# Forgetting attention in pairs of heads with its key bias by DRAM and GpSimd, and the S5 rotation on GpSimd

## The chip, the cores and the metric

The kernel runs on one core of a Trainium2 chip. Its time is the device time of one execution in microseconds (us), given as the median of several executions. A core has a matrix engine (PE, TensorE; its weight loads are shown apart as PEld), three elementwise engines (DVE or VectorE, ACT or ScalarE, POOL or GpSimd) and a queue engine (SP) that here issues every DMA. Each engine runs its own instruction list in order and waits on semaphores for the others. SBUF is the on-chip memory, PSUM the matrix engine's accumulators, DRAM the memory outside.

## The reference, cut to what matters

The network has three blocks on 256 tokens of width 1024. The change touches the third block's mixer, which adds three branches: forgetting attention ("fox"), a state-space recurrence ("s5") and a gated recurrence ("hgrn"). Fox has 8 heads of 64 features; its score gets a bias from a running sum of log forget gates, and is causal:

```python
c = jnp.cumsum(log_f, axis=1)                     # per head
s = jnp.einsum('bqhd,bkhd->bhqk', qi, k) * scale
s = s + ci[..., None] - c_keys                    # query bias, minus key bias
s = jnp.where(k_pos[None, :] <= q_pos[:, None], s, -jnp.inf)
p = jax.nn.softmax(s, axis=-1)
return jnp.einsum('bhqk,bkhd->bqhd', p, v)
```

The recurrence of s5 is complex, state by state, over the 256 tokens:

```python
h[t] = abar * h[t-1] + bbar @ u[t]                # complex
y[t] = Re(c @ h[t])
```

## The kernel before, in words

Weights are loaded in units of 1 MB into a tile `raw` (three buffers). ACT writes the high part `wh`, DVE the remainder `wl` (method `unit`, lines 366, 360, 351 are the helpers that issue matmul, tensor_tensor and activation), and PE does three products for each, `wh` with the high and the low part of the activations and `wl` with the high part. A unit is 48 products of 256 columns. These products are most of the kernel.

The mixer of the third block (`mixer2`) writes the steps of `M2_ORDER`, "su fox hz hv g2 g0 b0 glu dr g1 b1 b2": the projections, and between them side generators (fox, hgrn, s5) that are advanced a piece at a time. A scheduler puts the instructions of each engine into one fixed order when the kernel is built. Projections accumulate in PSUM tiles `mm`, everything else in four tiles `ax`.

**s5.** 16 groups of 128 states, two groups (`j`) in each of 8 steps (`p`). Per group: PE makes the drive `dp` (tile `ax<-su,s5bt`; the two groups sit in different 32-row strips); DVE multiplies it by cos and sin tables (`s5tl`, loaded from DRAM), adds, and scans the real and the imaginary part along time (`s5w<-mag,merged`), which is a recurrence in a rotating frame. Then the result is rotated back, one 128x512 product with sin into `merged` and one with cos in place in `s5w`, both on DVE. After every second step PE multiplies the four groups with the output matrix `s5c` (`ax<-s5w,s5c`, `ax<-merged,s5c`).

**fox.** The log gates and their running sum `c` live on 32 partitions (tiles `fr`); `cn` is its negative, `cc` holds `c` turned so that the query is on the partitions. Head by head (`step(h)`): for the query tiles t=0 (128 keys) and t=1 (256 keys), PE makes the scores (`ax<-fx`, 64 rows of contraction) and adds the key bias by a second product of 32 rows (`ax<-fr,cst`, a row of the identity against `cn`). ACT adds the query bias and copies to SBUF tile `qt`; DVE adds the causal mask and takes the row maximum in one instruction (line 1636); ACT does exp; DVE scales; PE transposes the probabilities (`ax<-cst,qt`) and multiplies them with the values (`ax<-qt,fx`, 64 columns of output). `lagged` issues the scores of a head before the transposes of the head before it. `qt` has four buffers.

PE's weights for a product on 64 or 32 rows fill only part of the array; products in different row strips or column strips can stand side by side in it.

Of the kernel before, what the change touches and what calls it, by code (L numbers as in the profile page):

```python
# [11 lines left out]
F32 = mybir.dt.float32  # L12
F32R = mybir.dt.float32r
I32 = mybir.dt.int32
AF = mybir.ActivationFunctionType
ALU = mybir.AluOpType
# [3 lines left out]
P = 128  # L20
D = 1024
T = 256
# [246 lines left out]
class Stack:  # L269
# [1109 lines left out]
    def s5(self, us):  # L1379

        nc = self.nc
        bt = self.pt("s5bt", [P, 2, 4, P])
        nc.sync.dma_start(out=bt.rearrange("p a b c -> p (a b c)"), in_=self.s5bt)
        cc = self.pt("s5c", [P, 3, 16, 32])
        nc.sync.dma_start(out=cc[:, 0:2].rearrange("p a b c -> p (a b c)"), in_=self.a["c5"])
        self.act(cc[:, 2], cc[:, 0], scale=-1.0)
        self.act(cc[:, 1], cc[:, 1], scale=-1.0)
        held = []

        def step(p):  # L1390


            f = p // 2
            u = us[f // 2][:, f % 2]
            js = (2 * p, 2 * p + 1)
            tabs, dps = [], []
            for j in js:
                tab = self.pt("s5tl", [P, 2, T], bufs=2)
                nc.sync.dma_start(out=tab, in_=self.s5tab[j].rearrange("p (a b) -> p a b", a=2))
                tabs.append(tab)  # L1400
                dps.append(self.ax((P, 2, T)))
            first = None
            for c in range(2):
                for j, dp in zip(js[::-1], dps[::-1]):
                    b = 32 * (j % 4)
                    first = self.after(first, self.matmul(dp[:, c], bt[b:b + 32, c, f], u[b:b + 32]))
            for j, tab, dp in zip(js, tabs, dps):
                w1 = self.pt(f"merged{j % 4}", [P, 2, T])
                w2 = self.pt("s5w2", [P, 2, T], bufs=4)
                cob = tab[:, 0].unsqueeze(1).to_broadcast([P, 2, T])  # L1410
                sib = tab[:, 1].unsqueeze(1).to_broadcast([P, 2, T])
                self.tt(w1, dp, cob, ALU.mult)
                self.tt(w2, dp, sib, ALU.mult)
                self.tt(w1[:, 0], w1[:, 0], w2[:, 1], ALU.add)
                self.tt(w1[:, 1], w1[:, 1], w2[:, 0], ALU.subtract)
                mg = self.mag[:, j:j + 1].to_broadcast([P, T])
                for c in range(2):
                    self.scan(w2[:, c], mg, w1[:, c], 0.0, ALU.mult, ALU.add)
                self.tt(w1, w2, sib, ALU.mult)
                self.tt(w2, w2, cob, ALU.mult)  # L1420
                held.append((j, w1, w2))

        def outputs(f):
            u = us[f // 2][:, f % 2]
            yp = self.ax((P, 512))[:, 0:T]

            first = None
            for i in range(4):
                for j, w1, w2 in held[::-1]:
                    b = 32 * (j % 4)  # L1430
                    c, w = ((0, w2[:, 0]), (2, w1[:, 1]), (1, w1[:, 0]), (1, w2[:, 1]))[i]
                    first = self.after(first, self.matmul(yp[b:b + 32], cc[:, c, j], w, i == 0, i == 3))
            held.clear()
            self.stt(u, u, self.col("s5d", f), yp, ALU.mult, ALU.add)

        for p in range(8):
            step(p)
            yield
            if p % 2:
                outputs(p // 2)  # L1440
            yield

        zh = self.pt("s5bt", [P, 4, T], F32R)
        zl = self.pt("s5c", [P, 4, T], F32R)
        a_ = []
        for i in range(2):
            y = us[i]
            a = self.pt("s5w2", [P, 2, T], bufs=4)
            a_.append(a)
            self.tt(a, y, y, ALU.mult)  # L1450
            self.ts(a, a, 0.044715 * GELU_C, GELU_C, ALU.mult, ALU.add)
            self.tt(a, a, y, ALU.mult)
            self.act(a, a, AF.Tanh)
            self.ts(a, a, 0.5, 0.5, ALU.mult, ALU.add)
            self.tt(y, y, a, ALU.mult)
            self.split(zh[:, 2 * i:2 * i + 2], zl[:, 2 * i:2 * i + 2], y)
        self.s5z = (zh, zl, us, a_)
        yield
# [145 lines left out]
    def fox(self, qkv):  # L1604
        nc = self.nc
        fp = self.ax()[0:32, 0:T]
        self.proj_rows("ff", fp)
        z, lf, na, c, cn = (self.pt(f"fr{i}", [32, T]) for i in range(5))
        self.ts(z, fp, self.col("fb", rows=32), None, ALU.add)
        self.log_sigmoid(lf, z, na)  # L1610
        self.scan(c, self.ones[0:32], lf, 0.0, ALU.mult, ALU.add)
        self.ts(cn, c, -1.0, None, ALU.mult)
        cp = self.ax((P, 4, P))
        for t in range(2):
            self.transpose(cp[:, t, 0:32], c[:, t * P:(t + 1) * P])
        cc = self.pt("fcc", [P, 2, 32])
        self.act(cc, cp[:, 0:2, 0:32])
        yh, yl = self.pt("fyh", [P, 4, T], F32R), self.pt("fyl", [P, 4, T], F32R)
        yield
        yp = []  # L1620

        def step(h):
            if len(qkv) < 3 * (h // 4) + 3:
                return True
            q, k, v = qkv[3 * (h // 4):3 * (h // 4) + 3]
            b, f = 64 * (h % 2), (h % 4) // 2
            sp = self.ax((P, 2, T))
            s = self.qt([P, 2, T])
            m, nm, su, rs = (self.sm(2, f"fs{i}") for i in range(4))
            for t in range(2):  # L1630
                w = (t + 1) * P
                mask = self.mB[:, P:] if t == 0 else self.mB
                self.matmul(sp[:, t, 0:w], q[b:b + 64, f, t * P:(t + 1) * P], k[b:b + 64, f, 0:w], True, False)
                self.matmul(sp[:, t, 0:w], self.ident[0:32, h:h + 1].to_broadcast([32, P]), cn[:, 0:w], False, True)
                self.act(s[:, t, 0:w], sp[:, t, 0:w], AF.Identity, bias=cc[:, t, h:h + 1])
                nc.vector.tensor_tensor_reduce(out=s[:, t, 0:w], in0=s[:, t, 0:w], in1=mask, scale=1.0, scalar=-3.0e38,
                                               op0=ALU.add, op1=ALU.max, accum_out=m[:, t:t + 1])
            self.ts(nm, m, -1.0, None, ALU.mult)
            for t in range(2):
                w = (t + 1) * P  # L1640
                self.act(s[:, t, 0:w], s[:, t, 0:w], AF.Exp, bias=nm[:, t:t + 1], accum_out=su[:, t:t + 1])
            nc.vector.reciprocal(out=rs, in_=su)

            def rest():
                tp = self.ax((P, 2, T))
                for t in range(2):
                    w = (t + 1) * P
                    self.ts(s[:, t, 0:w], s[:, t, 0:w], rs[:, t:t + 1], None, ALU.mult)
                    for kt in range(t + 1):
                        self.transpose(tp[:, kt, t * P:(t + 1) * P], s[:, t, kt * P:(kt + 1) * P])  # L1650
                pt = self.qt([P, 2, T])
                self.act(pt[:, 0], tp[:, 0])
                self.act(pt[:, 1, P:], tp[:, 1, P:])
                if h % 2 == 0:
                    yp.append(self.ax()[:, 0:T])
                hs = slice((h % 4) * 64, (h % 4 + 1) * 64)
                y = yp[-1]
                self.matmul(y[b:b + 64], v[:, 0, hs], pt[:, 0], True, False)
                self.matmul(y[b:b + 64, P:], v[:, 1, hs], pt[:, 1, P:], False, True)
                if h % 2:  # L1660
                    self.split(yh[:, h // 2], yl[:, h // 2], y)
            return rest

        yield from self.lagged([partial(step, h) for h in range(8)])
        self.yb[0] = (yh, yl)

    def mixer2(self, tick, nb=1):
# [275 lines left out]
```

## Time and profile before

| | |
|---|---|
| median of 3 runs | 1518.69 us (1518.07 to 1520.74) |
| the profiled execution | 1525.01 us, span 1523.2 us |
| PE busy | 1458.0 us |
| PEld busy | 1311.8 us |
| DVE busy | 1163.0 us |
| ACT busy | 855.7 us |
| POOL busy | 4.5 us |

The span runs from the first to the last instruction of the profiled execution; 1.8 us of its own time lie outside. Everything below is read from that one execution, and times of the trace count from the start of the span. The third block's mixer lies between about 936 and 1260 us.

### The profile page before, as it was taken

To read this page: it belongs to the slowest core of one execution; us is meant where nothing else is said; L and a number is where in the kernel's file an instruction comes from. 1 tells how busy PE (TensorE), PEld (TensorE's weight loads), DVE (VectorE), ACT (ScalarE), POOL (GpSimd) and SP (SyncE) were. 2 spreads that over 40 slices of the span, in tenths; PEclk is the share of its full clock that TensorE was granted. 3 is DMA by queue.
4 is the path that set the end of the run, shared out by engine and by line. 5 is a ranking of instruction groups with operands and counts; after the bars stand their busy time and mean duration, and the time that the engine had idled before them with its cause. 6 is when DMAs were issued, how large, how long until landed. Compare 5 with 4: busy or idle time off the path is not lost.

```text
span 1523.2 us, 25378 instructions
## 1 busy us (share of the span) xinstructions
PE 1458.0 (96%) x9964; PEld 1311.8 (86%) x9964; DVE 1163.0 (76%) x2223; ACT 855.7 (56%) x1502; POOL 4.5 (0%) x24
## 2 busy tenths in 40 slices
PE   2998999999999899999999999999999999999999
PEld 2987887898998899998889989967889989799998
DVE  7788988877778896667988856958999887565555
ACT  4786774654556565545757665535455457444443
POOL 0000000000000000000000000000000000000000
PEclk8999999999999999999999999969999999999999
DMA  8755887487875794436676655522344365245552
GB/s 347 262 167 171 292 307 265 189 313 282 318 294 200 291 315 158 166 139 211 230 263 227 242 217 192 173 97 89 133 142 149 132 224 198 83 150 182 194 181 97
DMA packets 62058, 315.47 MB, mean 207 GB/s; under 512 B 6385, under 2 KB 15217, under 8 KB 28146
## 3 DMA queue, kind: packets, MB, share of 16 engines
q1 hardware_dynamic: 61938, 313.85, 57.9%
q8 instruction: 78, 1.28, 0.3%
q14 instruction: 42, 0.34, 0.1%
HBM read 304.77 MB, written 9.05 MB: 206 GB/s over the span
## 4 chain that ended last, share of the span: by engine, by line
PE 74%; DVE 14%; ACT 5%; DMA 5%; issue 2%; SPq 0%; ACTq 0%; DVEq 0%
PE mm L366 48%; PE ax L366 23%; DVE wl L360 3%; PE ax L370 2%; ACT xn L351 1%; DMA bp<-cs_d 1%; ACT wh L351 1%; DVE merged L360 1%; ACT nb L351 1%; DMA grow<-in_rows 1%; DVE acc L751 1%; DVE s5w L373 1%; DVE s5w L360 1%; DMA bp<-nM_d 1%; DMA x<-in_x 1%
## 5 line engine op out<-in xcount | busy, mean ns | idle before, releaser
L360 DVE TENSOR_TENSOR wl<-raw,wh 128x1024 fp32r<-128x1024 f32 x400 | 485.5, 1223 | 198.0 <-ACT wh L351 197.3
L351 ACT ACTIVATE wh<-raw 128x1024 fp32r<-128x1024 f32 x400 | 419.4, 1057 | 359.6 <-PE mm L366 209.4
L366 PE MATMUL mm<-xh,wh 128*128 128x256 f32 x1536 | 442.3, 288 | 5.7 <-ACT bp L351 3.1
L366 PE MATMUL mm<-xh,wl 128*128 128x256 f32 x1536 | 441.7, 288 | 5.6 <-DVE wl L360 5.6
L366 PE MATMUL mm<-xl,wh 128*128 128x256 f32 x1536 | 439.9, 286 | 0.0
L366 PEld LDWEIGHTS mm<-xh,wl 128*128 128x128 f32 x1536 | 298.0, 194 | 12.2 <-DVE wl L360 7.4
L366 PEld LDWEIGHTS mm<-xh,wh 128*128 128x128 f32 x1536 | 298.3, 194 | 11.4 <-ACT bp L351 3.3
L366 PEld LDWEIGHTS mm<-xl,wh 128*128 128x128 f32 x1536 | 298.2, 194 | 3.8 <-issue 2.0
L366 PE MATMUL mm<-wh,xh 128*128 128x256 f32 x496 | 143.9, 290 | 0.0
L366 PE MATMUL mm<-wl,xh 128*128 128x256 f32 x496 | 142.5, 287 | 0.5 <-DVE wl L360 0.5
L366 PE MATMUL mm<-wh,xl 128*128 128x256 f32 x496 | 141.7, 286 | 0.0
L366 PE MATMUL ax<-wh,mhh 128*128 128x512 f32 x256 | 102.4, 400 | 0.0
L366 PE MATMUL ax<-wl,mhh 128*128 128x512 f32 x256 | 101.4, 396 | 0.0
L366 PE MATMUL ax<-wh,mhl 128*128 128x512 f32 x256 | 101.3, 396 | 0.0
L366 PEld LDWEIGHTS mm<-wl,xh 128*128 128x128 f32 x496 | 95.8, 193 | 3.2 <-DVE wl L360 2.2
L366 PEld LDWEIGHTS mm<-wh,xh 128*128 128x128 f32 x496 | 95.7, 193 | 1.9 <-issue 1.2
L366 PEld LDWEIGHTS mm<-wh,xl 128*128 128x128 f32 x496 | 95.8, 193 | 1.0 <-issue 0.8
L366 PEld LDWEIGHTS ax<-wh,mhl 128*128 128x128 f32 x256 | 48.1, 188 | 11.9 <-DVE mhl L360 0.4
L366 PEld LDWEIGHTS ax<-wl,mhh 128*128 128x128 f32 x256 | 48.1, 188 | 10.9 <-issue 0.5
L366 PEld LDWEIGHTS ax<-wh,mhh 128*128 128x128 f32 x256 | 48.2, 188 | 10.7 <-ACT wh L351 0.5
L363 DVE SCALAR_TENSOR_TENSOR acc<-raw,cond,acc 128x1024 f32<-128x1024 f32 x28 | 35.8, 1278 | 8.1 <-DMA raw<-in_ada 7.9
L751 DVE CUSTOM_DVE_ANT_0 acc<-raw,crow 128x1024 f32<-128x1024 f32 x32 | 39.0, 1219 | 2.6 <-DMA raw<-in_ada 2.3
(490 smaller groups left out, 2543.2 us busy)
## 6 DMA issues: line engine op xcount, KB each, us to landing
raw<-in_wts SPq DMA_DIRECT2D x214, 1024.0 KB, 4.9
raw<-in_ada SPq DMA_DIRECT2D x48, 1024.0 KB, 5.6
nb<-in_nab SPq DMA_DIRECT2D x16, 256.0 KB, 5.8
grow<-in_rows SPq DMA_DIRECT2D x16, 256.0 KB, 6.0
bp<-cs_d SPq DMA_DIRECT2D x16, 256.0 KB, 5.2
s5tab<-s5t SPq DMA_DIRECT2D x16, 256.0 KB, 2.5
s5tl<-s5tab SPq DMA_DIRECT2D x16, 256.0 KB, 2.7
meml<-mem_d SPq DMA_DIRECT2D x2, 1024.0 KB, 5.2
```

The source lines that it names most:

```text
L351: return self.nc.scalar.activation(out=out, in_=in_, func=func, **kw)
L360: return self.nc.vector.tensor_tensor(out=out, in0=in0, in1=in1, op=op)
L363: return self.nc.vector.scalar_tensor_tensor(out=out, in0=in0, scalar=s, in1=in1, op0=op0, op1=op1)
L366: return self.nc.tensor.matmul(out, lhsT, rhs, start=start, stop=stop)
L370: return self.nc.tensor.transpose(out, in_, self.ident[0:k, 0:k])
L373: return self.nc.vector.tensor_tensor_scan(out=out, data0=d0, data1=d1, initial=init, op0=op0, op1=op1)
L751: nc.vector.tensor_tensor_reduce(out=acc, in0=w, in1=self.crow, scale=1.0, scalar=0.0, op0=ALU.mult, op1=ALU.add, accum_out=s8[:, j:j + 1])
```

## The change

Fox now works on pairs of heads (`pair(g)`, heads 2g and 2g+1). The key bias no longer is a PE product: `cn` is written to DRAM once (`cn_d`, 8 rows of 256), and for each head its row is read back to all 128 partitions (`fcb`, two buffers); ACT adds the query bias to it and writes `qt`; GpSimd adds the causal mask on the two 128x128 blocks on the diagonal; DVE adds scores and bias and takes the maximum in one instruction, which now reads the scores from PSUM. The scores of the two heads are issued alternately, head 1 (rows 64 to 127) before head 0 (rows 0 to 63), and so are the products with the values (columns 64 to 127, then 0 to 63). The pair's scores and softmax come in one piece, its transposes and value products in the next, and the following pair after that. In s5 the two products of the rotation back are issued on GpSimd.

```diff
-                self.tt(w1, w2, sib, ALU.mult)
-                self.tt(w2, w2, cob, ALU.mult)
+                for out, rot in ((w1, sib), (w2, cob)):
+                    nc.gpsimd.tensor_tensor(out=out, in0=w2, in1=rot, op=ALU.mult)
                 held.append((j, w1, w2))
...
-        z, lf, na, c, cn = (self.pt(f"fr{i}", [32, T]) for i in range(5))
+        z, lf, na = (self.pt(f"fr{i}", [32, T]) for i in range(3))
         self.ts(z, fp, self.col("fb", rows=32), None, ALU.add)
         self.log_sigmoid(lf, z, na)
+        c, cn = z, na
         self.scan(c, self.ones[0:32], lf, 0.0, ALU.mult, ALU.add)
         self.ts(cn, c, -1.0, None, ALU.mult)
+        cnd = self.tc.dram_tile([8, T], F32, name="cn_d")
+        nc.sync.dma_start(out=cnd, in_=cn[0:8])
...
-                self.matmul(sp[:, t, 0:w], q[b:b + 64, f, t * P:(t + 1) * P], k[b:b + 64, f, 0:w], True, False)
-                self.matmul(sp[:, t, 0:w], self.ident[0:32, h:h + 1].to_broadcast([32, P]), cn[:, 0:w], False, True)
-                self.act(s[:, t, 0:w], sp[:, t, 0:w], AF.Identity, bias=cc[:, t, h:h + 1])
-                nc.vector.tensor_tensor_reduce(out=s[:, t, 0:w], in0=s[:, t, 0:w], in1=mask, scale=1.0, scalar=-3.0e38,
-                                               op0=ALU.add, op1=ALU.max, accum_out=m[:, t:t + 1])
...
+                cb = self.pt("fcb", [P, T], bufs=2)
+                nc.sync.dma_start(out=cb, in_=cnd[h].partition_broadcast(P))
+                s = self.qt([P, 2, T])
+                for t in range(2):
+                    self.act(s[:, t, 0:(t + 1) * P], cb[:, 0:(t + 1) * P], AF.Identity, bias=cc[:, t, h:h + 1])
+                ends = s.rearrange("p t n -> p (t n)").rearrange("p (i n) -> p i n", n=P)[:, 0:4:3]
+                nc.gpsimd.tensor_tensor(out=ends, in0=ends, in1=self.mB[:, P:].unsqueeze(1).to_broadcast([P, 2, P]), op=ALU.add)
+                ss.append(s)
+                sp.append(self.ax((P, 2, T)))
             for t in range(2):
...
+                for i in (1, 0):
+                    b, w = 64 * i, (t + 1) * P
+                    first = self.after(first, self.matmul(sp[i][:, t, 0:w], q[b:b + 64, f, t * P:(t + 1) * P], k[b:b + 64, f, 0:w]))
...
                 for t in range(2):
                     w = (t + 1) * P
-                    self.ts(s[:, t, 0:w], s[:, t, 0:w], rs[:, t:t + 1], None, ALU.mult)
+                    nc.vector.tensor_tensor_reduce(out=s[:, t, 0:w], in0=sp[i][:, t, 0:w], in1=s[:, t, 0:w], scale=1.0, scalar=-3.0e38,
+                                                   op0=ALU.add, op1=ALU.max, accum_out=m[:, t:t + 1])
...
+            for kt in range(2):
+                for i in (1, 0):
+                    b, hs, w = 64 * i, slice((2 * f + i) * 64, (2 * f + i + 1) * 64), slice(kt * P, T)
+                    first = self.after(first, self.matmul(y[b:b + 64, w], v[:, kt, hs], pts[i][:, kt, w], kt == 0, kt == 1))
```

The built order shows what stands where. On PE, at the first scores of fox (`ax<-fx` scores, `ax<-fr,cst` key bias, then the first output products of s5), before:

```order
L370 MATMUL ax<-cst,qksq 128x128 x4
L366 MATMUL ax<-fx 128x128
L366 MATMUL ax<-fr_10690,cst 128x128
L366 MATMUL ax<-s5w_10809,s5c 32x256
L366 MATMUL ax<-s5w_10799,s5c 32x256
```

and at the same place after the change:

```order
L370 MATMUL ax<-cst,qksq 128x128 x4
L366 MATMUL ax<-fx 128x128 x2
L366 MATMUL ax<-fx 128x256 x2
L366 MATMUL ax<-s5w_10809,s5c 32x256
L366 MATMUL ax<-s5w_10799,s5c 32x256
```

The four score products of two heads stand together and the bias products are gone. Some 30 rows later on PE, where the softmax of the first pair is used (`ax<-cst,qt` transposes, `ax<-qt,fx` value products, `mm` projection products), after the change:

```order
L370 MATMUL ax<-cst,qt 128x128
L366 MATMUL mm<-xh,wh 128x256
L370 MATMUL ax<-cst,qt 128x128 x2
L366 MATMUL mm<-xl,wh 128x256
L366 MATMUL mm<-xh,wl 128x256
L366 MATMUL ax<-fx 128x128 x2
L366 MATMUL ax<-qt,fx 64x256 x2
L366 MATMUL ax<-qt,fx 64x128 x2
L366 MATMUL ax<-fx 128x256 x2
L366 MATMUL ax<-su_10329,s5bt 128x256 x4
```

Behind this place 96 projection products follow in one piece; between the first scores and here there are 14 in all. Before the change 21 projection products stood between the first scores and the drive products of the same s5 step, and 46 behind them.

On DVE, in the first step of s5 (`s5w<-mag,merged` scan, `merged<-s5w,s5tl` and `s5w<-s5w,s5tl` rotation back, `fr` gates of fox), before:

```order
L373 SCALAR_TENSOR_TENSOR s5w_10575<-mag,merged_10574 128x256 x2
L360 TENSOR_TENSOR merged_10584<-merged_10584,s5w_10585 128x256
L360 TENSOR_TENSOR merged_10574<-s5w_10575,s5tl 128x512
L373 SCALAR_TENSOR_TENSOR s5w_10585<-mag,merged_10584 128x256
L360 TENSOR_TENSOR s5w_10575<-s5w_10575,s5tl 128x512
L373 SCALAR_TENSOR_TENSOR s5w_10585<-mag,merged_10584 128x256
L356 TENSOR_SCALAR fr_10686<-ax,cols 32x256
L360 TENSOR_TENSOR merged_10584<-s5w_10585,s5tl 128x512
L363 SCALAR_TENSOR_TENSOR fr_10688<-fr_10686 32x256
L360 TENSOR_TENSOR s5w_10585<-s5w_10585,s5tl 128x512
L360 TENSOR_TENSOR wl<-raw,wh 128x1024 x2
```

and after:

```order
L373 SCALAR_TENSOR_TENSOR s5w_10575<-mag,merged_10574 128x256 x2
L360 TENSOR_TENSOR merged_10584<-merged_10584,s5w_10585 128x256
L356 TENSOR_SCALAR fr_10686<-ax,cols 32x256
L373 SCALAR_TENSOR_TENSOR s5w_10585<-mag,merged_10584 128x256 x2
L363 SCALAR_TENSOR_TENSOR fr_10688<-fr_10686 32x256
L360 TENSOR_TENSOR wl<-raw,wh 128x1024
```

The four rotations left DVE's list, and fox's gates and the next `wl` moved up. They stand on POOL, whose list after the change is four rotations for each s5 step, the masks of fox (two instructions for a pair) between them, and one memset pair that hgrn's scan waits for.

## Rows read from the trace of the kernel before

**Rows 1.** The page, part 1: busy us, share of the span, instructions

```profile
PE 1458.0 (96%) x9964; PEld 1311.8 (86%) x9964; DVE 1163.0 (76%) x2223; ACT 855.7 (56%) x1502; POOL 4.5 (0%) x24
```

**Rows 2.** Windows: stretch, its us, busy of each engine, PEclk, DMA share

```profile
960.00:1002.40 42.40, 40.24 (x329) 37.76 (x331) 38.66 (x78) 19.56 (x27) 0.00 (x0) 1.00 0.47 161
1002.40:1033.10 30.70, 30.70 (x112) 18.78 (x101) 10.52 (x29) 14.78 (x30) 0.00 (x0) 0.50 0.14 53
1033.10:1100.00 66.90, 66.20 (x472) 53.89 (x471) 62.33 (x140) 31.89 (x68) 0.00 (x0) 1.00 0.37 123
1100.00:1160.00 60.00, 56.27 (x475) 51.64 (x473) 55.21 (x82) 28.62 (x34) 1.09 (x2) 0.97 0.37 127
1160.00:1215.00 55.00, 54.13 (x452) 53.50 (x453) 49.22 (x81) 27.41 (x34) 0.00 (x0) 1.00 0.41 145
```

**Rows 3.** Chain that ended last, around the first scores: start us, us, what

```profile
999.78 0.70 DVE qksq L360
...
1000.62 0.63 PE ax L370 x4
1001.25 7.94 PE ax L366 x44
```

**Rows 4.** Timeline of PE, second head of fox: start us, us

```profile
1007.67 0.79 PE L366 MATMUL ax<-fx 64*128 64x128 f32 x2
1008.40 0.79 PE L366 MATMUL ax<-fr,cst 32*128 32x128 f32 x2
...
1011.12 1.22 PE L366 MATMUL ax<-fx 64*128 64x256 f32 x2
1012.27 1.22 PE L366 MATMUL ax<-fr,cst 32*128 32x256 f32 x2
...
1015.10 1.54 PE L366 MATMUL ax<-qt,fx 128*64 128x256 f32 x4
```

**Rows 5.** Timeline of PE, later heads of fox and drives of s5

```profile
1062.94 0.86 PE L366 MATMUL ax<-qt,fx 128*64 128x256 f32 x4
...
1068.61 1.13 PE L366 MATMUL ax<-su,s5bt 32*128 32x256 f32 x8
...
1085.42 0.49 PE L366 MATMUL ax<-fx 64*128 64x128 f32 x2
1085.84 0.48 PE L366 MATMUL ax<-fr,cst 32*128 32x128 f32 x2
...
1086.96 0.70 PE L366 MATMUL ax<-fx 64*128 64x256 f32 x2
1087.59 0.69 PE L366 MATMUL ax<-fr,cst 32*128 32x256 f32 x2
...
1089.22 0.69 PE L366 MATMUL ax<-su,s5bt 32*128 32x256 f32 x2
```

**Rows 6.** Groups of DVE by shape, 936 to 1250 us: busy us, mean ns

```profile
L360 DVE TENSOR_TENSOR wl<-raw,wh 128x1024 fp32r<-128x1024 f32 x75 | 90.9, 1220 | 20.9 <-ACT wh L351 20.8
L373 DVE TENSOR_TENSOR_SCAN s5w<-mag,merged 128x256 f32<-128x256 f32 x32 | 20.8, 678 | 0.0
L360 DVE TENSOR_TENSOR merged<-merged,s5w 128x256 f32<-128x256 f32 x32 | 12.2, 414 | 0.0
L360 DVE TENSOR_TENSOR merged<-s5w,s5tl 128x512 f32<-128x512 f32 x16 | 11.0, 685 | 0.0
L360 DVE TENSOR_TENSOR s5w<-s5w,s5tl 128x512 f32<-128x512 f32 x16 | 10.9, 680 | 0.0
```

**Rows 7.** Timeline of POOL: two of its memsets

```profile
783.95 0.53 POOL L1350 MEMSET s5bb<- 128x512 f32 x1 [86.75 <-PE mm L370]
...
1111.36 0.96 POOL L1510 MEMSET xn<- 128x1024 f32 x1 [174.99 <-DVE xn L360]
```

**Rows 8.** DMA issues, 936 to 1110 us: count, KB, median us to landing

```profile
s5tl<-s5tab SPq DMA_DIRECT2D x14, 256.0 KB, 2.7
```

More of the change, by code (lines that the diff above doesn't have):

```diff
@@ L1619, in fox @@
         yield
[L1620 to L1629, printed above, removed]
-            for t in range(2):
-                w = (t + 1) * P
-                mask = self.mB[:, P:] if t == 0 else self.mB
-                self.matmul(sp[:, t, 0:w], q[b:b + 64, f, t * P:(t + 1) * P], k[b:b + 64, f, 0:w], True, False)
-                self.matmul(sp[:, t, 0:w], self.ident[0:32, h:h + 1].to_broadcast([32, P]), cn[:, 0:w], False, True)
-                self.act(s[:, t, 0:w], sp[:, t, 0:w], AF.Identity, bias=cc[:, t, h:h + 1])
-                nc.vector.tensor_tensor_reduce(out=s[:, t, 0:w], in0=s[:, t, 0:w], in1=mask, scale=1.0, scalar=-3.0e38,
-                                               op0=ALU.add, op1=ALU.max, accum_out=m[:, t:t + 1])
[L1638 to L1645, printed above, removed]
@@ new lines, in pair @@
+        def pair(g):
+            q, k, v = qkv[3 * (g // 2):3 * (g // 2) + 3]
+            f = g % 2
+            sp, ss, pts, first = [], [], [], None
+            for i in range(2):
+                h = 2 * g + i
+                cb = self.pt("fcb", [P, T], bufs=2)
[7 more added lines that the diff above has]
+                sp.append(self.ax((P, 2, T)))
+            for t in range(2):
+                for i in (1, 0):
+                    b, w = 64 * i, (t + 1) * P
+                    first = self.after(first, self.matmul(sp[i][:, t, 0:w], q[b:b + 64, f, t * P:(t + 1) * P], k[b:b + 64, f, 0:w]))
+            rss = []
+            for i in range(2):
+                s = ss[i]
+                m, nm, su, rs = (self.sm(2, f"fs{i}") for i in range(4))
@@ L1646, in rest @@
                 for t in range(2):
                     w = (t + 1) * P
-                    self.ts(s[:, t, 0:w], s[:, t, 0:w], rs[:, t:t + 1], None, ALU.mult)
+                    nc.vector.tensor_tensor_reduce(out=s[:, t, 0:w], in0=sp[i][:, t, 0:w], in1=s[:, t, 0:w], scale=1.0, scalar=-3.0e38,
+                                                   op0=ALU.add, op1=ALU.max, accum_out=m[:, t:t + 1])
+                self.ts(nm, m, -1.0, None, ALU.mult)
+                for t in range(2):
+                    w = (t + 1) * P
+                    self.act(s[:, t, 0:w], s[:, t, 0:w], AF.Exp, bias=nm[:, t:t + 1], accum_out=su[:, t:t + 1])
@@ L1649, in rest @@
+                nc.vector.reciprocal(out=rs, in_=su)
+                rss.append(rs)
+            yield
+            for i in range(2):
+                s, tp = ss[i], sp[i]
+                for t in range(2):
+                    w = (t + 1) * P
+                    self.ts(s[:, t, 0:w], s[:, t, 0:w], rss[i][:, t:t + 1], None, ALU.mult)
                     for kt in range(t + 1):
@@ L1653, in rest @@
                 self.act(pt[:, 1, P:], tp[:, 1, P:])
[L1654 to L1664, printed above, removed]
+                pts.append(pt)
+            first = None
+            y = sp[0][:, 0]
+            for kt in range(2):
+                for i in (1, 0):
+                    b, hs, w = 64 * i, slice((2 * f + i) * 64, (2 * f + i + 1) * 64), slice(kt * P, T)
+                    first = self.after(first, self.matmul(y[b:b + 64, w], v[:, kt, hs], pts[i][:, kt, w], kt == 0, kt == 1))
+            self.split(yh[:, g], yl[:, g], y)
+            yield
+        for g in range(4):
+            while len(qkv) < 3 * (g // 2) + 3:
+                yield True
+            yield from pair(g)
         self.yb[0] = (yh, yl)
```

## The prediction

> **What bounds the kernel now.** I read the page's busy shares first: PE is busy 96% of the span, DVE 76%, POOL not at all [rows 1]. So a change in the third mixer is worth what it does to PE's time there, or to the waits of PE. Then the stretches of that mixer [rows 2]. From 960 to 1002.4 DVE is busy 38.66 of 42.4 us and PE is idle 2.2. [...] From 1033.1 to 1215 both are near full: PE idle 0.7, 3.7 and 0.9 us, DVE idle 4.6, 4.8 and 5.8, or 15.2 in all. The chain of waits shows the hinge [rows 3]: DVE's last normalisation before fox ends at 1000.5, PE waits for it, and then runs one piece of scores and s5 outputs; the clock falls 1 to 2 us later. What the engine did before it fell was to wait for DVE, and then products on 32 or 64 rows or columns.
>
> **PE's scores.** At the lower clock a head of fox costs 0.73 us for each product of 128 columns (1007.67 to 1008.40) and 1.15 for each of 256 (1011.12 to 1012.27) [rows 4]. A head has one of each for the scores and one of each for the key bias: 3.76 us. At the full clock the starts are 0.42 and 0.63 apart [rows 5]: 2.10 us. In the slow stretch lie two whole heads and the 256-column half of the first: 2 x 3.76 + 2.30 = 9.8 us. At the full clock lie five heads and 0.84: 11.3. Together 21.1 us of PE.
>
> After it the bias products are gone, and two heads' scores stand side by side on rows 0 to 63 and 64 to 127. The nearest row for products side by side is the drive of s5, which has that form already: four products (8 instructions) of 256 columns take 1.13 us, and one alone takes 0.69 [rows 5]. That is 1.13 against 2.76, a ratio of 0.41. So the scores of a pair, 2.1 us one after the other (two heads of 1.05), cost 0.86 us at the full clock and 1.54 at the lower. With two pairs at each clock: 4.8 us. **Term 1: 21.1 - 4.8 = -16.3 us.** Bound on the other side: nothing overlaps, 2 x 3.76 + 2 x 2.10 = 11.7, and the term is -9.4.
>
> **PE's value products.** A head's two take 1.54 us at the lower clock [rows 4] and 0.86 at the full one [rows 5]: 2 x 1.54 + 6 x 0.86 = 8.2. Two heads now go to different column halves of the array. Bounds: no overlap 0, the drive's ratio of 0.41 -4.8; I take a half, since the weights of these products are another shape than the drive's. **Term 2: -4.1 us.**
>
> **The clock.** What is left in the slow stretch after terms 1 and 2 is 30.7 - 9.8 - 3.1 = 17.8 us at the lower level. The built order puts a dense run of 96 projection products behind pair 1, where 46 stood, but only 14 instead of 21 ahead of it, so PE is given short pieces and waits for the first pair's softmax there, as now. If the clock stays high throughout, 8.9 us come back; if it falls in a second place of this length, as much and more goes. I count **term 3: 0**, with 9 us both ways.
>
> **DVE's rotations.** The 32 rotations take 11.0 + 10.9 = 21.9 us of DVE [rows 6]. POOL gets them, and eight masks of 256 elements. No row shows POOL doing a tensor_tensor. From below: DVE's 0.69 us. From above: POOL's memset of 128x512 writes one stream in 0.53 us [rows 7]; two inputs and an output one after the other would be 1.6. I take the middle, 1.1 us. [...]
>
> For a step of s5 the chain hardly changes: four rotations of 1.1 us on POOL begin when the first group's scans end, and the second group's scans (two of 0.68 and an addition of 0.41, [rows 6]) run meanwhile, so 4.4 - 1.8 = 2.6 us remain behind the last scan, where DVE needs about 1.4 now. That is 1.2 us later, but DVE reached the scan a rotation (0.69 us) sooner: 0.5 us net. Behind the rotations in POOL's list stand the masks, then DVE's maximum, and hgrn's memset. PE takes outputs of s5 at four places: **term 4: +2 us**. At 0.69 us a rotation it is 0 to -1, at 1.6 it is +10.
>
> **What DVE lets through.** Behind 1033.1 PE's part of terms 1 and 2 is 10.5 - 1.7 (heads of the full-clock part, against two pairs) + 2.6 = 11.4 us. DVE is idle only 15.2 of 182 us there, and its waits are not where PE needs them, so I let it take back half: **term 5: +5.8 us**. For this I let the 21.9 us that DVE loses count for nothing: the order was built for them, and in the rivals below they count with either sign.
>
> **The rest at nothing.** The nine small DMAs land in some 2.7 us each (the nearest, of 256 KB, [rows 8]) and move 1 MB, against a DMA share of 0.14 to 0.47 in these stretches [rows 2]; the chain gates, write, read, ACT, mask is 2.7 + 2.7 + about 2 us and starts some 20 us before the first scores. Without that cover the first pair would be 5 us late. On SP's queue the reads stand behind one another and the next weight unit behind them; raw has three buffers, so a unit late by 2.7 us is not seen, or costs these 2.7 once. ACT's sixteen copies are as many as before, only from SBUF and earlier. DVE's maximum reads PSUM in place of SBUF, the same count.
>
> **The sum.** -16.3 - 4.1 + 0 + 2 + 5.8 = -12.6 us. The profiled execution took 1525.0 us (span 1523.2 and 1.8 around it), 6.3 above the median of the runs, so it should come to 1512.4 when profiled alike, and the median from 1518.7 to **1506 us**.
>
> **The rivals.**
> *More comes through.* DVE's 21.9 us are real room: term 5 is not taken back, and the 2.2 us that PE waits for DVE up to 1002.4 vanish. For it: DVE is the fuller engine in three of five stretches. Against it: the order is fixed and other waits come last. -16.3 - 4.1 + 2 - 2.2 = -20.6 us, 1498.
>
> *GpSimd holds DVE up (slower).* In this kernel nearly all that DVE does beside the rotations reads two tiles of SBUF: `wl`, scans, additions [rows 6]. If such a row can't run while POOL reads, each rotation costs DVE up to its own length: 32 x 1.1 + 8 x 0.6 = 40 us of POOL, against 21.9 saved. Up to 1002.4, two steps at 4 x (1.1 - 0.69) = 1.6 us lose 3.4; behind 1033.1 all of PE's 11.4 us are lost; and POOL's rows wait for `wl` of 1.2 us in turn, so each of the four outputs of s5 comes some 3 us late, +12. Then -20.4 + 3.4 + 11.4 + 12 = +6.4 us, 1525. It decides from 2.5 us of lost PE time for each of the eight steps. For it: DVE's list is dense there, so some row is always held. Against it: four of the twelve rows left in a step read PSUM and one tile, and no row of this trace has both engines at work, so nothing here shows it. [...]
>
> *The softmax of a pair is waited for, and the clock stays low longer.* Before, a head's scores went ahead of the transposes of the head before it; now a pair's scores, softmax and transposes follow each other, with 9 projection products (1.9 us at the lower clock) between. DVE's maxima, ACT's exp and DVE's scaling are some 5 us for a pair. With 3 us lost at each of two pairs and 4 us more at the lower clock, -12.6 + 10 = -3 us, 1516. The slow stretch of before speaks for it; the dense run of 96 behind it against.
>
> **How the numbers follow.** The forecast has a chance of 0.38, more coming through 0.20, the long softmax and low clock 0.18, GpSimd holding DVE up 0.24. A measurement of this kernel tells about 0.2%, 3 us, from no change. The forecast and the first rival are faster; the softmax case is faster with 0.08 and the same with 0.10; GpSimd's case is slower. So faster 0.66, same 0.10, slower 0.24. For eight in ten the range goes from 1495 (the first rival, with the clock a little better) to 1526 (GpSimd's case); the faster cases alone span 1495 to 1514.
>
> **What would show it.** Term 1: no bias products, and 8 score instructions of a pair within about 0.9 us (or 1.6 at the lower clock). Term 2: the four value products of a pair near 1 us. Term 3: the length of the stretch with PEclk 0.50 around 1000, now 30.7 us. Term 4: POOL rows of L1420 near 1.1 us, and PE's wait ahead of the first `s5c` product, by POOL. Term 5: DVE's busy share behind 1033. GpSimd's case would show as longer means of `wl<-raw,wh` (now 1220 ns), of the scans (678) and the additions (414), and a new stretch with a low clock. The prediction is wrong if the rotation on POOL takes 2 us or more, if PE waits over 2 us at each s5 output, or if the low clock comes back in a second place.

## The result, and the profile after

The changed kernel takes 1539.92 us (median; 1537.98 to 1544.78), the kernel before 1518.51 beside it: a ratio of 1.0139, with a 95% interval of 1.0114 to 1.0163. It is slower by 1.4%, where 1506 us was forecast with a range up to 1526. The profiled execution after took 1540.74 us, its span is 1539.0.

Part 1 of the page after, the same line as in [rows 1] (busy us, share of the span, instructions):

```profile
PE 1439.3 (94%) x9932; PEld 1304.1 (85%) x9932; DVE 1175.3 (76%) x2191; ACT 853.9 (55%) x1502; POOL 72.7 (5%) x64
```

PE is busy for 18.7 us less than before (1458.0 to 1439.3): that side of the change came. But the span grew by 15.8 us, from 1523.2 to 1539.0, so PE's idle time grew by 34.5, from 65.2 to 99.7 us. And DVE, which lost 32 rotations of 21.9 us, is busy 12.3 us *longer*. The groups by shape show where, first DVE's from 936 to 1270 us after (columns as in [rows 6]):

```profile
L360 DVE TENSOR_TENSOR wl<-raw,wh 128x1024 fp32r<-128x1024 f32 x76 | 101.2, 1340 | 28.0 <-ACT wh L351 27.7 <-PE ax L366 0.2
L373 DVE TENSOR_TENSOR_SCAN s5w<-mag,merged 128x256 f32<-128x256 f32 x32 | 30.8, 1002 | 0.1
L360 DVE TENSOR_TENSOR merged<-merged,s5w 128x256 f32<-128x256 f32 x32 | 14.0, 478 | 0.0
L360 DVE TENSOR_TENSOR merged<-ax,s5tl 128x512 f32<-128x512 f32 x16 | 10.5, 683 | 0.3 <-PE ax L366 0.3
...
L356 DVE TENSOR_SCALAR qt<-qt,fs 128x128 f32<-128x128 f32 x8 | 5.1, 635 | 0.1
```

Against [rows 6], `wl` went from 1220 to 1340 ns, the scans from 678 to 1002, the additions from 414 to 478. The scaling of the softmax (`qt<-qt,fs`, 128 columns) took 276 ns in the trace of before and takes 635. The product that reads PSUM, `merged<-ax,s5tl`, kept its 683 ns. These two rows before, 936 to 1270 us:

```profile
L360 DVE TENSOR_TENSOR merged<-ax,s5tl 128x512 f32<-128x512 f32 x16 | 10.7, 683 | 3.1 <-PE ax L366 3.0
L356 DVE TENSOR_SCALAR qt<-qt,fs 128x128 f32<-128x128 f32 x8 | 2.2, 276 | 0.1
```

POOL's groups in the same stretch:

```profile
L1420 POOL TENSOR_TENSOR merged<-s5w,s5tl 128x512 f32<-128x512 f32 x16 | 33.4, 2088 | 103.1 <-DVE s5w L373 81.8 <-issue 20.7 <-DVE qkr4v L357 0.6
L1420 POOL TENSOR_TENSOR s5w<-s5w,s5tl 128x512 f32<-128x512 f32 x16 | 27.5, 1717 | 1.3
L1638 POOL TENSOR_TENSOR qt<-qt,cst 128x256 f32<-128x256 f32 x8 | 7.4, 948 | 36.9 <-ACT qt L351 36.9
```

A rotation product takes 2.1 us (by the sine) or 1.7 (by the cosine) on the mean, not the 1.1 that I took. One step of s5 shows both engines at it. DVE's timeline (start us, us):

```profile
1025.72 1.27 DVE L373 TENSOR_TENSOR_SCAN s5w<-mag,merged 128x256 f32<-128x256 f32 x2
...
1027.22 1.22 DVE L360 TENSOR_TENSOR wl<-raw,wh 128x1024 fp32r<-128x1024 f32 x1
1028.35 2.32 DVE L373 TENSOR_TENSOR_SCAN s5w<-mag,merged 128x256 f32<-128x256 f32 x2
1030.60 4.11 DVE L356 TENSOR_SCALAR qt<-qt,fs 128x128 f32<-128x128 f32 x4
```

and POOL's beside it:

```profile
1027.07 3.06 POOL L1420 TENSOR_TENSOR merged<-s5w,s5tl 128x512 f32<-128x512 f32 x1 [5.60 <-DVE s5w L373]
1030.21 1.56 POOL L1420 TENSOR_TENSOR s5w<-s5w,s5tl 128x512 f32<-128x512 f32 x1
1031.72 1.30 POOL L1420 TENSOR_TENSOR merged<-s5w,s5tl 128x512 f32<-128x512 f32 x1
1033.10 1.27 POOL L1420 TENSOR_TENSOR s5w<-s5w,s5tl 128x512 f32<-128x512 f32 x1
```

POOL's first rotation is 3.06 us long, beside `wl` and a scan of DVE; the second pair of scans is 1.05 us longer than the first; then four scalings (two of 128 and two of 256 columns, though the row names one shape) that took 1.2 us together before, by their means of 276 and 348 ns, take 4.11, beside three more rotations. Neither engine waits for a semaphore there: the time is inside the rows. What PE then waits for, from 936 to 1270 us (us in total, times, longest):

```profile
PE ax L366 <- POOL s5w L1420: 17.6, 3, 9.0
PE ax L370 <- DVE qt L356: 5.7, 2, 4.7
PE ax L370 <- DVE qksq L360: 4.2, 3, 3.6
PE ax L370 <- DVE fr L373: 4.1, 1, 4.1
PE ax L366 <- ACT qt L351: 3.3, 1, 3.3
```

Half of it is for the outputs of s5: 4.5, 4.0 and 9.0 us at three of the four. The rest is for other work of DVE that came late, and 3.3 us for ACT. Before, the largest of these waits was that for `wl`, and none was for s5:

```profile
PE mm L366 <- DVE wl L360: 3.2, 2, 2.5
```

In windows of 10 us after (columns as in [rows 2]):

```profile
980.00:990.00 10.00, 7.47 (x43) 7.43 (x44) 7.32 (x15) 2.99 (x5) 1.76 (x2) 0.66 0.49 175
...
1000.00:1010.00 10.00, 4.08 (x31) 3.70 (x31) 9.20 (x14) 0.36 (x1) 5.90 (x3) 0.92 0.31 104
1010.00:1020.00 10.00, 10.00 (x80) 6.07 (x78) 4.39 (x18) 7.38 (x21) 0.22 (x1) 0.74 0.39 160
...
1050.00:1060.00 10.00, 5.48 (x44) 3.09 (x43) 9.72 (x16) 5.31 (x15) 7.50 (x5) 0.66 0.68 221
...
1090.00:1100.00 10.00, 9.47 (x42) 7.16 (x43) 9.47 (x17) 4.51 (x10) 0.52 (x2) 0.52 0.23 94
1100.00:1110.00 10.00, 5.96 (x50) 5.75 (x53) 10.00 (x8) 2.61 (x3) 7.83 (x4) 0.97 0.35 132
1110.00:1120.00 10.00, 10.00 (x88) 8.43 (x83) 5.02 (x6) 3.24 (x4) 0.00 (x0) 0.83 0.37 133
...
1140.00:1150.00 10.00, 4.11 (x35) 3.90 (x33) 9.96 (x15) 2.12 (x2) 4.53 (x3) 0.92 0.56 222
1150.00:1160.00 10.00, 6.89 (x52) 4.70 (x53) 5.06 (x8) 0.42 (x1) 2.98 (x2) 0.57 0.33 107
```

In four of these windows (from 1000, 1050, 1100 and 1140) POOL is busy for 4.5 to 7.8 us, DVE for 9.2 to 10, and PE stands still for 4 to 6; in them or right behind them the mean granted clock of PE falls (to 0.74 from 1010, 0.66 from 1050, 0.83 from 1110 and 0.57 from 1150). Before it was one stretch of 30.7 us at 0.50 [rows 2], the prediction's slow stretch; now it is several short ones.

### The profile page after: what moved, and what is told of

Its sections match the earlier page's. It is cut to its first block, busy times and chain, and to the rows that moved or that the text cites. A ratio compares the mean times of both kernels' runs of the same rounds, so it can differ in the third digit from the quotient of the medians.

```text
span 1539.0 us, 25403 instructions
## 1 busy us (share of the span) xinstructions
PE 1439.3 (94%) x9932; PEld 1304.1 (85%) x9932; DVE 1175.3 (76%) x2191; ACT 853.9 (55%) x1502; POOL 72.7 (5%) x64
## 5 line engine op out<-in xcount | busy, mean ns | idle before, releaser
L360 DVE TENSOR_TENSOR wl<-raw,wh 128x1024 fp32r<-128x1024 f32 x400 | 494.4, 1245 | 206.2 <-ACT wh L351 205.2
L366 PEld LDWEIGHTS ax<-wh,mhh 128*128 128x128 f32 x256 | 48.2, 188 | 10.7 <-ACT wh L351 0.5
L751 DVE CUSTOM_DVE_ANT_0 acc<-raw,crow 128x1024 f32<-128x1024 f32 x32 | 39.0, 1218 | 2.6 <-DMA raw<-in_ada 2.3
```

What stands on the lines that cost most here:

```text
L360: return self.nc.vector.tensor_tensor(out=out, in0=in0, in1=in1, op=op)
L366: return self.nc.tensor.matmul(out, lhsT, rhs, start=start, stop=stop)
L751: nc.vector.tensor_tensor_reduce(out=acc, in0=w, in1=self.crow, scale=1.0, scalar=0.0, op0=ALU.mult, op1=ALU.add, accum_out=s8[:, j:j + 1])
```

## The experiments

**The theory (A):** while a GpSimd instruction reads SBUF, DVE rows whose inputs all lie in SBUF are held up, and the other way round; both engines' rows lengthen, the outputs of s5 and DVE's other results come late, PE waits, and its clock falls. **Rivals:** (B) the work on pairs costs it, since a pair's softmax is waited for; (C) GpSimd's own length and the longer chain of s5 cost it, without any holding up. Idle time of PE and mean granted clock are for the window 960 to 1240 us of each profile, which holds somewhat different work in each; the means of `wl` and of the scans are from 936 to 1270. Each version is built anew, so the order of the instructions can change with it.

| kernel | us, median | ratio to before, 95% | PE idle | PEclk | `wl`, scan ns |
|---|---|---|---|---|---|
| before | 1518.5 | | 8.2 | 0.94 | 1220, 678 |
| changed | 1539.9 | 1.0114 to 1.0163 | 38.4 | 0.91 | 1340, 1002 |
| 1 changed, rotations on DVE | 1514.8 | 0.995 to 0.999 | 19.5 | 0.98 | 1221, 680 |
| 2 before, rotations on GpSimd | 1557.6 | 1.0222 to 1.0283 | 29.9 | 0.90 | 1355, 970 |
| 3 as 1, masks on DVE too | 1509.3 | 0.9899 to 0.9955 | 15.3 | 0.98 | 1221, 683 |
| 4 changed, rotations only write | 1498.2 | 0.9833 to 0.9887 | 11.0 | 0.99 | 1220, 677 |
| 5 changed, half of the rotations | 1523.7 | 1.0012 to 1.0055 | 25.5 | 0.96 | 1239, 915 |
| 7 as 3, scaling on ACT | 1504.6 | 0.9882 to 0.9929 | 13.9 | 0.99 | 1218, 675 |
| 8 pairs alone, bias on PE | 1511.4 | 0.9918 to 0.9970 | 10.7 | 0.98 | 1217, 674 |

**1. The rotations back on DVE.**

```diff
-                for out, rot in ((w1, sib), (w2, cob)):
-                    nc.gpsimd.tensor_tensor(out=out, in0=w2, in1=rot, op=ALU.mult)
+                self.tt(w1, w2, sib, ALU.mult)
+                self.tt(w2, w2, cob, ALU.mult)
```

> The changed kernel with the 32 rotations of s5 back on DVE; fox on pairs with its bias by DRAM and the masks on GpSimd stay. Theory A (GpSimd's rotations read SBUF and hold DVE's rows up, and are themselves held up): nearly all of the loss goes, DVE's wl rows are back near 1220 ns, scans near 680, and the time is 1503 to 1512 us, under the kernel before. Rival B (the pairs cost it: a pair's softmax is waited for and the clock falls): the time stays at 1530 to 1542, with the low clock around the pairs. Rival C (GpSimd's own length in the chain of s5, no holding up): also 1503 to 1512; the memset run tells C from A.

Measured 1514.84 us. The rows are back at their lengths (`wl` 1221 ns, scans 680) and the loss is gone, so B is out: the pairs do not cost 20 us. The time is 3 us above the range given, which run 3 takes up.

**2. Only the rotations moved.**

```diff
-                self.tt(w1, w2, sib, ALU.mult)
-                self.tt(w2, w2, cob, ALU.mult)
+                for out, rot in ((w1, sib), (w2, cob)):
+                    nc.gpsimd.tensor_tensor(out=out, in0=w2, in1=rot, op=ALU.mult)
```

> The kernel before with only the 32 rotations moved to GpSimd; heads of fox one by one with the bias products on PE, as before. Theory A: wl rows near 1340 ns and scans near 1000 as in the changed kernel, PE waits for the s5 outputs at its four places, 1535 to 1555 us (the loss of the change, without the 20 us that the pairs take off PE). Rival B: within 5 us of the kernel before. Rival C: 1525 to 1540, with DVE's rows at their old length.

Measured 1557.64 us: 39 us slower than the kernel before, by this edit and the order built with it, and 18 slower than the changed kernel. DVE's rows lengthen as there (`wl` 1355 ns, scans 970), against what C expects, and the time lies 3 us above A's range. The gain of the pairs depends on what stands beside them: 18 us here, 4 with the rotations on DVE (run 1).

**3. Nothing on GpSimd that reads SBUF.**

```diff
-                nc.gpsimd.tensor_tensor(out=ends, in0=ends, in1=self.mB[:, P:]...
+                nc.vector.tensor_tensor(out=ends, in0=ends, in1=self.mB[:, P:]...
```

(run 1 with this besides)

> The changed kernel with rotations and masks on DVE, so that no GpSimd instruction reads SBUF in the third mixer. Theory A: as the run with the rotations on DVE alone, within 3 us of it (eight masks of 0.7 us held DVE up by about 5 us, and cost it about 3 now): 1503 to 1512. Rival B: 1530 to 1542.

Measured 1509.26 us, in the range and faster than the kernel before, but 5.6 under run 1 where at most 3 were expected (the two intervals just touch). That eight masks of 0.95 us on GpSimd cost more than that is only partly explained: DVE's maxima wait 3.1 us for them in run 1, and none of that is left here. PE's waits of this run, 936 to 1270 us, show what is left:

```profile
PE mm L366 <- DVE wl L360: 9.2, 6, 4.7
PE ax L370 <- DVE qt L356: 1.7, 3, 0.6
```

The softmax of a pair is waited for 1.7 us in all; PE waits most for DVE's `wl`, 9.2 us.

**4. In place of the rotations, writes that read nothing.**

```diff
-                for out, rot in ((w1, sib), (w2, cob)):
-                    nc.gpsimd.tensor_tensor(out=out, in0=w2, in1=rot, op=ALU.mult)
+                for out in (w1, w1, w2, w2):
+                    nc.gpsimd.memset(out, 0.0)
```

> The changed kernel in the same order on every engine, but each rotation on GpSimd is replaced by two memsets of its output (the rotation is left out): GpSimd's work keeps its place and its dependencies, lasts about 1.1 us for each rotation and writes SBUF, but reads nothing. Theory A (reading is what excludes): DVE's rows are back at wl 1220, scans 680, adds 414 ns, the s5 outputs come some 2 to 4 us sooner at each place, and the time is 1500 to 1515. Rival C (the dependence on GpSimd alone delays s5): 1525 to 1540. If DVE's rows stay as long as in the changed kernel, writing excludes as well as reading.

The eight masks stay on GpSimd and still read SBUF (7.0 us in all). The dependencies are those of the changed kernel, and the order is nearly that: by the two traces 8 rows of DVE, all behind 1080 us, and 25 products of PE stand a few us from their old places, and some rows of ACT and DMA issues too. Measured 1498.23 us, 42 us less. Groups of DVE and POOL from 936 to 1270 us:

```profile
L360 DVE TENSOR_TENSOR wl<-raw,wh 128x1024 fp32r<-128x1024 f32 x82 | 99.6, 1220 | 27.7 <-ACT wh L351 27.4 <-PE ax L366 0.2
L373 DVE TENSOR_TENSOR_SCAN s5w<-mag,merged 128x256 f32<-128x256 f32 x32 | 20.3, 677 | 0.1
...
L356 DVE TENSOR_SCALAR qt<-qt,fs 128x128 f32<-128x128 f32 x8 | 3.4, 422 | 0.1
...
L1420 POOL MEMSET merged<- 128x512 f32 x32 | 17.1, 535 | 100.7 <-DVE s5w L373 66.1 <-issue 34.3 <-DVE qkr4v L357 0.2
```

With the dependence on GpSimd kept and 34 us of its work, the loss is gone and `wl` and scans have their old lengths (1220 and 677 ns): the reading of the rotations is what costs, and C is out as the main cause. (GpSimd's part is also shorter here, two memsets of 0.53 us for a rotation product of 1.26 alone, 6 us over the 32; what this gives was not separated from the 42.) One thing was not as expected: the scaling rows, which read a single tile, stay longer than 276 ns.

**5. Half of the rotations.**

```diff
-                for out, rot in ((w1, sib), (w2, cob)):
-                    nc.gpsimd.tensor_tensor(out=out, in0=w2, in1=rot, op=ALU.mult)
+                self.tt(w1, w2, sib, ALU.mult)
+                nc.gpsimd.tensor_tensor(out=w2, in0=w2, in1=cob, op=ALU.mult)
```

> The changed kernel with the first product of each rotation (by the sine) back on DVE and only the second (by the cosine, in place) on GpSimd: 16 of the 32 instructions move. Theory A (the loss goes with the time in which GpSimd reads SBUF): about half of the 25 us between the run with the rotations on DVE (1514.8) and the changed kernel (1539.9), so 1522 to 1532, with wl near 1280 ns and scans near 840. Rival C (that the chain of s5 ends on GpSimd is what costs, however much is done there): 1535 or more.

Measured 1523.7 us, in A's range and outside C's. 16 rotations of 1.69 us cost 9 us over run 1, the other 16 a further 16. The scans are longer than expected (915 ns) and `wl` shorter (1239): which row is hit seems to depend on what stands beside the rotation; this was not followed further.

**6 and 9. The rows by themselves.** Behind the end of the kernel before stand twelve rows of 128x512 in each pairing.

```diff
+        blocks = [("ttalone", tt(V, a), None, None), ("tsalone", ts(V, a), None, None), ("rotalone", None, tt(G, a), None),
+                  ("ttrot", tt(V, a), tt(G, a), None), ("tsrot", ts(V, a), tt(G, a), None),
+                  ("psttrot", tt(V, ps), tt(G, a), None), ("pstsrot", ts(V, ps), tt(G, a), None),
+                  ("ttset", tt(V, a), ms, None), ("tsset", ts(V, a), ms, None),
+                  ("cprot", None, tt(G, a), cp), ("cpalone", None, None, cp)]
```

(`tt` is a product with a second tile `pb`, `ts` a product with a number, V is DVE, G is GpSimd, `ps` a PSUM tile, `ms` a memset on GpSimd, `cp` a copy on ACT.)

> The kernel before with a block of plain rows of 128x512 behind its end, one pairing of engines after the other, to price the terms by themselves. Theory A: GpSimd's product of two SBUF tiles alone takes 1.1 to 1.4 us; beside DVE products of two SBUF tiles both engines' rows lengthen to about the sum of the two (1.8 to 2.2 us for a pair); DVE rows that read PSUM and one tile, or PSUM alone, and ACT's rows keep their length (0.68, 0.4 and 0.5 us), memsets lengthen nothing that reads two tiles. Of DVE rows that read one SBUF tile beside a GpSimd product I expect that they lengthen too (128 columns went from 276 to 635 ns in the changed kernel), also beside a memset (422 ns in the run with writes only). Rival: all rows keep their lengths, and what was seen came from other causes (DMA traffic, PSUM).

In this first form the scheduler ran pairings into each other, so that only some rows can be read: GpSimd's product took 1.26 us beside ACT's copies, which took 0.63 us, and beside DVE rows on PSUM, which took 0.68 to 0.69. The second form keeps the pairings apart.

> The rows of the first probe again behind the end of the kernel before, with each pairing kept apart from the next by data (in the first probe two pairings ran into each other). Theory A, sized from the first probe (rows alternated there at 1.40 us for a GpSimd product and one DVE row on one tile, 1.67 for one on two tiles): GpSimd's product alone paces at 1.05 to 1.25 us; beside DVE rows on two tiles both engines advance by one row each in 1.67 us, beside rows on one SBUF tile in 1.40; beside DVE rows that read PSUM (with or without one tile), and beside ACT's copies, all keep the pace they have alone (0.61, 0.61 and 0.56 us); DVE rows on two tiles keep 0.61 beside memsets, rows on one tile go from 0.34 to about 0.6. Rival: DVE waits for GpSimd but not GpSimd for DVE (GpSimd's pace stays as alone in every pairing).

The rows of single tiles in its trace (ns of one: shortest, median, longest; first and last start):

```profile
L1874 DVE TENSOR_TENSOR ttalone_V<-pa,pb x12: 691/692/693, 1517.1 to 1525.1; 128x512 f32<-128x512 f32 x12
L1877 DVE TENSOR_SCALAR tsalone_V<-pa x12: 363/427/428, 1526.9 to 1532.2; 128x512 f32<-128x512 f32 x12
L1874 POOL TENSOR_TENSOR rotalone_G<-pa,pb x12: 1262/1262/1262, 1534.9 to 1549.6; 128x512 f32<-128x512 f32 x12
L1874 DVE TENSOR_TENSOR ttrot_V<-pa,pb x12: 692/1633/1636, 1552.4 to 1569.8; 128x512 f32<-128x512 f32 x12
L1874 POOL TENSOR_TENSOR ttrot_G<-pa,pb x12: 1262/1590/1591, 1554.3 to 1572.6; 128x512 f32<-128x512 f32 x12
L1877 DVE TENSOR_SCALAR tsrot_V<-pa x12: 364/1366/1366, 1575.3 to 1589.7; 128x512 f32<-128x512 f32 x12
L1874 POOL TENSOR_TENSOR tsrot_G<-pa,pb x12: 1262/1322/1322, 1576.9 to 1592.3; 128x512 f32<-128x512 f32 x12
L1874 DVE TENSOR_TENSOR psttrot_V<-ax,pb x12: 627/691/692, 1595.0 to 1614.0; 128x512 f32<-128x512 f32 x12
L1874 DVE TENSOR_TENSOR ttset_V<-pa,pb x12: 666/692/1428, 1635.2 to 1646.2; 128x512 f32<-128x512 f32 x12
L1877 DVE TENSOR_SCALAR tsset_V<-pa x12: 364/707/1361, 1648.1 to 1656.6; 128x512 f32<-128x512 f32 x12
L1879 POOL MEMSET tsset_G<- x12: 524/684/687, 1649.6 to 1657.8; 128x512 f32 x12
L1880 ACT ACTIVATE cprot_A<-pa x12: 629/629/631, 1659.3 to 1666.6; 128x512 f32<-128x512 f32 x12
```

A rotation alone takes 1262 ns, and eleven start in 14.7 us, one each 1.34 (1.05 to 1.25 was expected; the other rows alone are slower than expected too). Beside it a DVE product of two SBUF tiles goes from 692 to 1633 ns, and the rotation itself to 1590, one each 1.66 us (18.3 for eleven). Both engines are held up, so the rival of run 9, that only DVE waits, is out for these rows. The 1.66 us are what run 9 expected, but less than the 1.8 to 2.2 of run 6, and less than the 1.95 that the two rows alone add up to (692 and 1262): some 0.3 us of each pair still overlap. A DVE row on a single SBUF tile goes from 427 to 1366, while the rotation beside it goes only from 1262 to 1322, one each 1.40 us (15.4 for eleven): here it is nearly DVE alone that waits, as the rival has it. A row that reads PSUM and one tile stays at 691 (ten of the twelve ran beside rotations), ACT's copy at 629. Beside memsets a row on two tiles stays at 692, one on a single tile goes to 707 (about 600 was expected).

**7. The scaling on ACT.** A version that uses the finding: once GpSimd is quiet, PE waits most for DVE (9.2 us for `wl` in run 3), so some of DVE's work goes to ACT, which was busy for 144 us of the 280 from 960 to 1240 there, where DVE was for 252.

```diff
-                    self.ts(s[:, t, 0:w], s[:, t, 0:w], rss[i][:, t:t + 1], None, ALU.mult)
+                    self.act(s[:, t, 0:w], s[:, t, 0:w], scale=rss[i][:, t:t + 1])
```

> The run without GpSimd reads (1509.3), with the scaling of the softmax rows by the reciprocal sum on ACT in place of DVE (16 rows, 5 us of DVE). If DVE is what bounds this mixer once GpSimd is quiet (the write-only run was 16.6 us faster for 21.9 us off DVE), about 3 to 4 us come off: 1504 to 1508. If DVE's room is taken back by waits elsewhere: 1508 to 1512.

Measured 1504.55 us, as expected of a DVE-bound stretch: the fastest complete version, 0.95% under the kernel before. Against run 3 it is 4.7 us, and the two intervals overlap.

**8. Pairs alone.**

```diff
-                    first = self.after(first, self.matmul(sp[i][:, t, 0:w], q[b:b + 64, f, t * P:(t + 1) * P], k[b:b + 64, f, 0:w]))
+                    first = self.after(first, self.matmul(sp[i][:, t, 0:w], q[b:b + 64, f, t * P:(t + 1) * P], k[b:b + 64, f, 0:w], True, False))
+                for i in (1, 0):
+                    h, w = 2 * g + i, (t + 1) * P
+                    self.matmul(sp[i][:, t, 0:w], self.ident[0:32, h:h + 1].to_broadcast([32, P]), cn[:, 0:w], False, True)
...
+                    self.act(s[:, t, 0:w], sp[i][:, t, 0:w], AF.Identity, bias=cc[:, t, 2 * g + i:2 * g + i + 1])
```

> Pairs alone: the rotations on DVE, scores and value products of two heads side by side, but the key bias as products on PE and mask and maximum on DVE in one row, as before; no DRAM path, no masks on GpSimd. It splits term 1: the bias products are left (4 for each head, 10 us of PE over the eight at the two clocks; 4.2 at the full clock for four pairs). Theory: 3 to 8 us slower than the run without GpSimd reads, 1512 to 1518. Rival (the loss of the lag between heads costs as much as the pairing gives, and what the run without GpSimd reads gained came from the bias path alone): 1519 or more.

Measured 1511.38 us, just under the range of the theory and 2 us above run 3 with intervals that overlap. The rival is out: the pairing alone is faster than before. The bias products are 8.5 us of PE here (5.4 and 3.1 by shape), and run 3, which is without them but has 3.3 us of mask rows on DVE besides, is at most some 2 to 3 us faster. That PE's time is not what ends last there is the likely reading; the two effects were not separated.

## Why the prediction was wrong

**What held.** *Term 1*, -16.3 us: all score and bias products took 23.2 us of PE before (7.1, 7.1, 4.5 and 4.5 by shape) and 5.3 after (3.0 and 2.3), -17.9. A pair's scores take 0.93 us at the full clock, where 0.86 was forecast; the bound without any overlap is excluded. PE's timeline after:

```profile
1048.71 0.93 PE L366 MATMUL ax<-fx 64*128 64x128 f32 x8
...
1065.89 0.87 PE L366 MATMUL ax<-qt,fx 128*64 128x256 f32 x8
```

*Term 2*, -4.1: the value products went from 9.9 to 5.6 us, 0.87 for a pair. "The rest at nothing" held as far as DMAs go: no row of PE's waits, after or in run 3, names one. The case of the softmax of a pair is refuted by runs 3 and 8 as a cause of its own: PE waits 1.7 us for `qt` of DVE in run 3, and the 5.7 of after came with the rotations. In run 3, which is the change without GpSimd, PE is busy for 1433.2 of 1507.3 us: 24.8 less than before, with 8.9 more of idle time, where term 5 put down 5.8 for what DVE does not let through. Its 1509.3 us lie 3 above the forecast, so the fox half of the sum came out near the mark.

**The step that failed** is in *term 5*, "I let the 21.9 us that DVE loses count for nothing", and with it *term 4*: that a rotation on GpSimd costs DVE nothing and is itself not held up. The two terms allowed for 7.8 us of PE's time; PE's idle time grew by 34.5, since rows of DVE and of GpSimd lengthen beside each other (in run 9 from 692 to 1633 and from 1262 to 1590 ns). Both signs are now measured apart. DVE's relief, with the rotations' reads gone (the masks stay), is worth 16.6 us (run 1 to run 4, in different built orders); the reading of the 32 rotations costs 42 us (run 4 to the changed kernel, in nearly the same order). Neither is nothing, and they don't cancel. The prediction had the right place for this, the rival *GpSimd holds DVE up*, and gave it 0.24. The argument held against it, that no row of the trace has both engines at work, was true and no evidence. The rival's condition, that a DVE row on two SBUF tiles can't run while GpSimd reads, was an assumption that no row of the kernel before shows. Run 9 shows which rows are hit: beside a rotation a row on two SBUF tiles goes from 692 to 1633 ns, one with an input in PSUM stays at 691, ACT's copy at 629; beside memsets a row on two tiles stays at 692. But they were not kept apart for the whole row: a pair takes 1.66 us where the two rows add up to 1.95. And a row on a single SBUF tile, which the rival does not name, goes from 427 to 1366 ns there, and from 276 to 635 for the softmax scaling in the changed kernel.

**Why that rival came out at 1525 and not at 1540.** It put 26.8 us of waiting and lost gain on PE (3.4, 11.4 and 12); PE's idle time grew by 34.5, so 7.7 more. Behind this stand the rotation's price, taken at 1.1 us (alone it takes 1.26, in its place 1.7 to 2.1), and PE's waits: 17.6 us for outputs of s5, where 12 were put down, and 14.0 for `qt`, `qksq` and `fr`, of which the rival had only the 3.4 up to 1002. It took -20.4 for PE's work against the -18.7 seen, 1.7 more. And it came to a median by way of a profiled execution that was 6.3 us above its median, where that of after is 0.8 above: 5.5 more. 7.7 + 1.7 + 5.5 is 14.9, the whole difference. (Two roundings in the prediction, half of 11.4 as 5.8 and two steps of 1.6 as 3.4, change nothing.)

*Term 4*, +2, was wrong with it. Of the marks that the prediction set, the product by the sine passed 2 us (2.09) and that by the cosine did not (1.72), and PE waited more than 2 us at three of the four outputs. *Term 3*, 0: the one stretch at the lower clock went, but others came; the mean PEclk of 960 to 1240 is 0.91 against 0.94. By these two means that is some 8 us of PE at full speed over the 280 us, an estimate. In all runs that have pairs and no reading rotations on GpSimd (1, 3, 4, 7 and 8) it is 0.98 or 0.99, by the same estimate some 11 to 14 us more than before: the pairs, with the order built for them, give the clock back, and the reading rotations take it away (0.91 in the changed kernel, 0.90 in run 2). PE's idle time alone doesn't tell the clock: run 1 idles for 19.5 us at 0.98, the kernel before for 8.2 at 0.94, with a slow stretch in which PE never idled. How the clock and the waits share the loss was not separated.

*More comes through*, the other rival, names what run 4 shows: if GpSimd had been harmless, 1498 us; run 4 took 1498.2 with the rotation left out. That the two agree so closely is in part luck: the rival's sum has nothing for the clock, which went from 0.94 to 0.99 there, and run 4's masks still read.

## What to carry to other kernels

Before work is moved from DVE to GpSimd, look at what DVE does beside it: rows with two SBUF tiles, and scalings on a single one, were held up beside a GpSimd read here (692 to 1633 ns and 427 to 1366). With two tiles, rows of 0.69 and 1.26 us then took 1.6 us each, on both engines, and the move was slower than leaving the work on DVE (by 25 us against run 1, by 39 in run 2) even though DVE was by far the fuller of the two (1163.0 us busy against 4.5 [rows 1]). What can leave DVE goes to ACT, whose copies kept their 629 ns beside rotations, and what GpSimd could do here without holding DVE up are memsets beside rows on two tiles (692 ns, as alone). A resource on which no row of the trace has two engines at work is unknown, not free: price it before the sum is made.

## What the runs showed of the hardware that was not expected

In run 9 a memset on GpSimd lengthened a DVE row on a single SBUF tile (427 to 707 ns, and the memset from 524 to 684), but not a row on two tiles (692). So what writes and what reads must be told apart for each form of DVE row.

In a mixed list the two engines did not take turns row by row. In the changed kernel the rotation at 1027.07 us started ahead of `wl` (1027.22), yet `wl` kept its 1.22 us and the scan behind it its 0.69, and the rotation took 3.06; only the next scan was held up, to 1.72. With rows on two tiles alone, in run 9, both engines started a row each 1.66 us.
